# A streaming-encoder layer on one core: the attention values with 64 weight columns, and part of a depthwise convolution as packed matrix products

## The chip, the cores and the metric

The kernel runs on one core of one Trainium2 chip. The metric is device time in microseconds (us) of one execution. A core has five engines with a queue each: TensorE (PE) for matrix products into PSUM banks, with its weight loads (PEld) listed apart; VectorE (DVE), ScalarE (ACT) and GpSimd (POOL) for elementwise work; and SyncE (SP), which issues most DMAs. Each engine takes its own instructions in order and waits on semaphores of the others. A PSUM bank is 128 partitions by 512 float32; of the eight, seven rotate under the name `ps` and one, `cv`, is the accumulator of a convolution.

## What is computed

The reference has 2 layers on 512 tokens of width 1024. A layer is a SwiGLU, a mixing block, and a second SwiGLU. The change is in the mixing block, which has an attention branch and a convolution branch:

```python
probs = jax.nn.softmax(scores, axis=-1)            # 8 heads, causal by chunks of 64 tokens
outs.append(jnp.einsum('bhqk,bhkd->bqhd', probs, vs))   # 64 values per head
...
a, g = u_raw[..., :CONV_W], u_raw[..., CONV_W:]    # CONV_W = 512 channels
u = a * jax.nn.sigmoid(g)
y = lax.conv_general_dilated(u, conv_w[:, None, :], window_strides=(1,),
        padding=[(CONV_K - 1, 0)], feature_group_count=CONV_W)   # CONV_K = 31 taps per channel
return jax.nn.silu(layer_norm(y + conv_b, ln_g, ln_b))
...
x = x + jnp.concatenate([attn, conv], axis=-1) @ w_out
```

All of it is float32 in and out, to float32 accuracy.

## The kernel before

Large products are made float32-accurate by splitting each operand into a rounded part (`fp32r`) and the rest, and adding three products of these (`mm3`, L154 to L156). Products of plain float32 operands appear as two matmul records each in the trace. Activations lie with features on partitions and tokens along the row, as tiles of 128x512.

The mixing block (`mix_body`) is written as stages. First the projections, in the order of `SEQ`: gated linear units for the four convolution groups c0 to c3 (`conv_in` and `glu`, L626 to L632, each leaving a tile `u[c]` of 128 channels by 512 tokens), latents for queries and keys, then the up-projections. In `SEQ` the keys (`uk`, DVE lines L777 to L785) stand ahead of c2 and c3. Then the attention goes in steps: in a step one head's q and k are transposed (`turn`, L811 and L816), another head's scores are made and exponentiated (`scores`, L834 to L840), another's probabilities are transposed (`turn_p`, L855 and L858), another's values are summed (`values`, L868), and finished pairs of heads are transposed back (`turn_out`, L886) and split for the output projection. In `values` the transposed probabilities are the weights (128 columns) and the 64 value columns stream past them: 10 products per head, then one DVE multiplication by the reciprocal sums for a pair of heads (L875).

The convolution has 4 groups of 128 channels with 31 taps each. `CONV = "DAAD"` gives groups 0 and 3 to DVE alone: 30 fused multiply-adds into the PSUM bank `cv` (L922), then an ACT copy to `u[c]`. Groups 1 and 2 go to ACT and POOL: ACT makes each tap's product (`pr`, L926) and POOL adds it to a sum `y` (L930). From tap 16 of group 1 on, these additions are issued only after the keys. POOL then sums the four groups (L944 to L946), TensorE takes their mean (L948), and the layer norm follows on DVE, ACT and POOL up to the products of the output projection. Its attention rows for the first three output tiles (`early_groups`, `WOG = 3`) run on TensorE meanwhile.

The order of instructions on an engine is set by a scheduler: it takes the program as written, with `tc.issue_after` as extra bounds, and places each instruction by its own estimate of times. So moving an instruction in the source can move others on its queue.

Of the kernel before, what the change touches and what calls it, by code (L numbers as in the profile page):

```python
# [7 lines left out]
FP = mybir.dt.float32  # L8
# [10 lines left out]
L = 2  # L19
# [27 lines left out]
GLUP = 0  # L47
EARLY = "s"
PRELOAD = 1
E1 = 0  # L50
YP = 1
E2 = 2
E3 = 3
WOG = 3
WAKE = 10
KS = (0, 2, 4, 6, 1, 3, 5, 7)
WOP = 4
# [2 lines left out]
JOINED = ("b21", "t3", "t4")  # L60

VECS = [("g1", 8), ("gm", 8), ("g2", 8), ("gp", 8), ("gql", 3), ("gkl", 2),
        ("cw", 4 * CK), ("cb", 4), ("lg", 4), ("lb", 4), ("gq", 1), ("gk", 1)]
VOFF = {}
_o = 0
for _n, _w in VECS:
# [1 line left out]
    _o += _w  # L68
VN = _o
CCOS, CSIN, CID = 0, 64, 128  # L70
CN = 256


@with_exitstack
def encoder_kernel(ctx: ExitStack, tc: tile.TileContext, xT, consts, vecs, rgain, wgu1, wd1, wdq1,
# [54 lines left out]
    def vv(l, name):  # L130
        o, w = VOFF[name]
        return vec[:, l, o:o + w]
# [483 lines left out]

    def mix_body(kpool, l, gx, norm, done):
        u, order = [], {}

        def kept(dt=FP):  # L620
            return kpool.tile([P, S], dt, tag="m", name=nm("m"), bufs=2 * WIDE)
        ys = [None if kind == "D" else kpool.tile([P, S], FP, tag="y", name=nm("y"), bufs=2) for kind in CONV]

        def glu(pa, pg):
            tg = tmp()
            V.tensor_tensor(tg, pg, R, ALU.mult)  # L626
            sg = tmp()
            order["gate"] = A.activation(sg, tg, AF.Sigmoid).ins
            ta = tmp()
            V.tensor_tensor(ta, pa, R, ALU.mult)  # L630
            uc = kept()
            (G if GLUP else V).tensor_tensor(uc, ta, sg, ALU.mult)  # L632
            u.append(uc)

        def conv_in(c):
            pp = []
            for j in range(2):
                ps = bank()
                group(ps, load_w(wcv[l, 2 * c + j], WC, f"c{c}"), gx, range(KD), KD)
                pp.append(ps)  # L640
            glu(*pp)

        gql, gkl = vv(l, "gql"), vv(l, "gkl")
        KW = KVL + DR
# [21 lines left out]
        def latent_k():  # L666

            pk = [bank() for _ in range(NT)]
            for k0 in range(0, KD, 3):
                n = min(3, KD - k0)  # L670
                wh, wl = load_w(wkl[l, :, k0 * KW:(k0 + n) * KW], n * KW, "k")
                for k in range(k0, k0 + n):
                    cs = slice((k - k0) * KW, (k - k0 + 1) * KW)
                    for t in range(NT):
                        ts_ = slice(t * P, (t + 1) * P)
                        mm3(pk[t][:, :KW], gx[k][0][:, ts_], gx[k][1][:, ts_], wh[:, cs], wl[:, cs],
                            k == 0, k == KD - 1)
            for t in range(NT):
                A.copy(ckl[t // 2][:, t % 2], pk[t][:, :KVL])
                A.copy(cke[:, t], pk[t][:, KVL:KW])  # L680
                j = tmp()
                A.activation(j[:, :KVL], pk[t][:, :KVL], AF.Square, accum_out=ssl[:, t:t + 1])
                j = tmp()
                A.activation(j[:, :DR], pk[t][:, KVL:KW], AF.Square, accum_out=sspe[:, t:t + 1])


        tabs = []
# [173 lines left out]
        def values(h):  # L861

            if h % 2 == 0:
                heads[h]["po"] = bank()
            po = heads[h - h % 2]["po"].rearrange("p (t h d) -> p t h d", t=NT, h=2)
            for t in range(NT):
                for j in range(t + 1):
                    T.matmul(po[:, t, h % 2], heads[h]["pt"][j][:, (t - j) * P:(t - j + 1) * P],  # L868
                             vs[j][:, h * DV:(h + 1) * DV], start=j == 0, stop=j == t)
            if h % 2 == 0:  # L870
                return
            rs = small.tile([P, NT, 2], FP, tag="rs", name=nm("rs"))
            V.reciprocal(rs, heads[h - 1]["sums"])
            o = tmp()
            V.tensor_tensor(o.rearrange("p (t h d) -> p t h d", t=NT, h=2), po,  # L875
                            rs[:, :, :, None].to_broadcast([P, NT, 2, DV]), ALU.mult)
            heads[h]["o"] = o

        def turn_out(h):

            if h % 2 == 0:
                return
            o = heads[h]["o"]
            ps = bank()
            for t in range(NT):
                T.transpose(ps[:, t * P:(t + 1) * P], o[:, t * P:(t + 1) * P], ident)  # L886
# [15 lines left out]
        with tc.issue_after(order["gate"]):  # L902
            scores(0)
        for step in range(H + 6):
            for stage, lag in STAGES:
# [8 lines left out]
        for c in range(4):  # L914
            kind = CONV[c]
            acc = psum.tile([P, S], FP, tag="cv", name=nm("cv"), bufs=1) if kind == "D" else ys[c]
            tap = lambda k: cw[:, c * CK + k:c * CK + k + 1]
            A.activation(acc, u[c], AF.Identity, scale=tap(CK - 1), bias=cb[:, c:c + 1])  # L918
            for k in range(CK - 2, -1, -1):
                s = CK - 1 - k  # L920
                if kind == "D":
                    V.scalar_tensor_tensor(acc[:, s:], u[c][:, :S - s], tap(k), acc[:, s:], ALU.mult, ALU.add)  # L922
                    continue
                pr = kpool.tile([P, S], FP, tag="pr", name=nm("pr"), bufs=3)
                if kind == "A":
                    A.activation(pr[:, s:], u[c][:, :S - s], AF.Copy, scale=tap(k))  # L926
                else:
                    G.tensor_scalar(pr[:, s:], u[c][:, :S - s], tap(k), None, ALU.mult)
                with tc.issue_after(order["keys"]) if s >= PAUSE or c > 1 else nullcontext():
                    order["conv"] = G.tensor_tensor(acc[:, s:], acc[:, s:], pr[:, s:], ALU.add).ins  # L930
            if kind == "D":
                A.copy(u[c], acc)
                ys[c] = u[c]
        early = []

        def early_groups(ms):
# [3 lines left out]
                    group(early[m], wo[m], at, range(4), KD)  # L940

        early_groups(range(E1))
        ysum = tmp()
        G.tensor_tensor(ysum, ys[0], ys[1], ALU.add)  # L944
        G.tensor_tensor(ysum, ysum, ys[2], ALU.add)
        (G if YP else V).tensor_tensor(ysum, ysum, ys[3], ALU.add)  # L946
        pm = bank()
        T.matmul(pm, onesm, ysum, start=True, stop=True)  # L948
        if PRELOAD:
# [291 lines left out]
```

## Time and profile before

| what | value |
|---|---|
| median of 3 runs | 1799.76 us (1798.87 to 1799.94) |
| the profiled execution, and its span | 1798.87 us, 1797.1 us |
| PE, PEld, DVE, ACT, POOL busy | 99%, 89%, 83%, 62%, 23% of the span |
| mixing block from the end of the c3 products to the first convolution product of the output projection | 442.4 to 521.4 us (layer 0), 1332 to 1411 us (layer 1) |
| TensorE clock granted | 1.00 throughout |

A matmul row of the timeline gives start and length of one or several records. Since products overlap in TensorE's pipeline, the distance from one start to the next, and not the listed length, is what a product takes. In a row `out<-in,in` of a matmul the first operand streams and the second is the weights.

### The profile page before, as it was taken

How to read it: one execution, taken by the hardware profiler on the slowest of the kernel's cores; microseconds unless marked ns; L12 is line 12 of the kernel's file. 1: busy time of each engine (PE TensorE's matmuls, PEld its weight loads, DVE VectorE, ACT ScalarE, POOL GpSimd, SP SyncE). 2: the span in 40 equal slices, each digit the busy share in tenths (PEclk: the TensorE clock that was granted, in tenths of full speed). 3: DMA queues.
4: the chain of work that ended last, by engine and by line, in shares of the span. 5: the costliest groups of instructions: out<-in, count | busy, mean ns of one | idle time of the engine just before them, and what ended most of it. 6: DMA issues, size and time to landing. Idle time of an engine off the chain costs nothing.

```text
span 1797.1 us, 29235 instructions
## 1 busy us (share of the span) xinstructions
PE 1781.8 (99%) x11334; PEld 1602.4 (89%) x11334; DVE 1494.5 (83%) x2299; ACT 1107.5 (62%) x1721; POOL 421.5 (23%) x343
## 2 busy tenths in 40 slices
PE   9999999999999999999999999999999999999998
PEld 7899999888788899999888999998978788999997
DVE  7898988589956989898779989876998668989883
ACT  5575756457953575756645757554779435756564
POOL 1000000258943000000310000002689410000002
PEclk9999999999999999999999999999999999999999
DMA  5657575325103466665426575743250125575742
GB/s 168 171 131 182 135 177 123 109 88 134 33 22 102 123 164 161 155 160 132 123 65 170 122 194 122 193 112 111 81 147 7 46 82 160 140 183 134 182 117 74
DMA packets 70413, 226.16 MB, mean 126 GB/s; under 512 B 7937, under 2 KB 8321, under 8 KB 70273
## 3 DMA queue, kind: packets, MB, share of 16 engines
q1 hardware_dynamic: 54000, 169.74, 30.3%
q0 software_dynamic: 16128, 54.53, 18.0%
q8 instruction: 89, 1.46, 0.3%
q14 instruction: 52, 0.42, 0.1%
q10 hardware_dynamic: 144, 0.00, 0.0%
HBM read 222.15 MB, written 2.10 MB: 125 GB/s over the span
## 4 chain that ended last, share of the span: by engine, by line
PE 91%; ACT 3%; DVE 2%; POOL 2%; issue 1%; DMA 0%; SPq 0%; ACTq 0%; POOLq 0%; DVEq 0%
PE ps L154 24%; PE ps L156 23%; PE ps L155 23%; PE ps L373 11%; PE ps L374 6%; PE ps L868 1%; PE ps L834 1%; POOL y L930 1%; ACT pr L926 1%; ACT r L840 1%; PE ps L855 1%; PE ps L198 0%; POOL sck L173 0%; PE ps L217 0%; DVE wl L246 0%
## 5 line engine op out<-in xcount | busy, mean ns | idle before, releaser
L155 PE MATMUL ps<-r,wh 128*128 128x256 f32 (+1 forms) x2540 | 806.8, 318 | 0.0
L154 PE MATMUL ps<-r,wh 128*128 128x256 f32 (+1 forms) x2540 | 803.6, 320 | 2.2 <-ACT wh L138 0.7
L156 PE MATMUL ps<-r,wl 128*128 128x256 f32 (+1 forms) x2348 | 749.2, 321 | 0.0
L154 PEld LDWEIGHTS ps<-r,wh 128*128 128x128 f32 x2540 | 480.5, 189 | 47.0 <-ACT wh L138 3.6
L155 PEld LDWEIGHTS ps<-r,wh 128*128 128x128 f32 x2540 | 481.6, 190 | 35.8 <-DVE r L162 1.5
L156 PEld LDWEIGHTS ps<-r,wl 128*128 128x128 f32 x2348 | 445.1, 190 | 33.5 <-DVE wl L144 0.4
L373 PE MATMUL ps<-xj,wh 128*128 128x512 f32 x864 | 303.9, 392 | 0.0
L138 ACT CAST wh<-raw 128x1024 fp32r<-128x1024 f32 (+3 forms) x148 | 131.9, 899 | 208.1 <-PE ps L155 125.8
L390 POOL DMA_DIRECT2D ls<-in_wgu x72 | 62.7, 871 | 734.7 <-ACT ls L389 595.3
L244 ACT CAST wh<-fr 128x1024 fp32r<-128x1024 f32 (+1 forms) x160 | 157.6, 985 | 104.4 <-DVE fr L410 53.2
L144 DVE TENSOR_TENSOR wl<-raw,wh 128x1024 fp32r<-128x1024 f32 (+3 forms) x132 | 145.3, 1108 | 91.3 <-ACT wh L138 90.9
L246 DVE TENSOR_TENSOR wl<-fr,wh 128x1024 fp32r<-128x1024 f32 (+1 forms) x160 | 182.3, 1139 | 20.3 <-ACT wh L244 20.3
L373 PEld LDWEIGHTS ps<-xj,wh 128*128 128x128 f32 x864 | 161.4, 188 | 30.1
L930 POOL TENSOR_TENSOR y<-y,pr 128x511 f32<-128x511 f32 (+14 forms) x120 | 158.6, 1322 | 54.5 <-ACT pr L926 47.1
L374 PE MATMUL ps<-xj,ls 128*128 128x256 f32 x576 | 161.3, 280 | 0.0
L244 ACT CAST wh<-raw 128x1024 fp32r<-128x1024 f32 (+1 forms) x100 | 98.2, 982 | 45.1 <-PE ps L155 24.2
L246 DVE TENSOR_TENSOR wl<-raw,wh 128x1024 fp32r<-128x1024 f32 (+1 forms) x100 | 113.5, 1135 | 14.2 <-ACT wh L244 13.7
L191 POOL TENSOR_TENSOR r<-r,t 128x512 f32<-128x512 f32 x45 | 75.0, 1676 | 175.6 <-ACT t L187 174.8
L374 PEld LDWEIGHTS ps<-xj,ls 128*128 128x128 f32 x576 | 108.3, 188 | 0.0
L389 ACT ACTIVATE ls<-fr 128x1024 fp32r<-128x1024 f32 (+1 forms) x56 | 56.1, 1002 | 74.5 <-PE ps L374 42.8
L926 ACT ACTIVATE pr<-m,vec 128x511 f32<-128x511 f32 (+14 forms) x120 | 85.7, 736 | 13.2 <-POOL y L930 13.2
L922 DVE SCALAR_TENSOR_TENSOR cv<-m,vec,cv 128x511 f32<-128x511 f32 (+14 forms) x120 | 87.8, 732 | 3.6 <-ACT cv L918 2.2
(241 smaller groups left out, 2944.9 us busy)
## 6 DMA issues: line engine op xcount, KB each, us to landing
fr<-in_wgu SPq DMA_DIRECT2D x112, 512.0 KB, 4.2
ls<-in_wgu POOLq DMA_DIRECT2D x72, 512.0 KB, 6.2
raw<-in_wgu SPq DMA_DIRECT2D x62, 512.0 KB, 4.5
fr<-in_wdq SPq DMA_DIRECT2D x48, 384.0 KB, 4.6
ls<-in_wdq POOLq DMA_DIRECT2D x32, 384.0 KB, 4.8
raw<-in_wd SPq DMA_DIRECT2D x32, 384.0 KB, 3.2
raw<-in_wd SPq DMA_DIRECT2D x32, 256.0 KB, 2.8
raw<-in_wcv SPq DMA_DIRECT2D x16, 512.0 KB, 3.6
```

The source lines that it names most:

```text
L138: order["cast"] = A.copy(hi[:, :w], raw[:, :w]).ins
L144: (G if kind in POOLW.split() else V).tensor_tensor(lo[:, :w], raw[:, :w], hi[:, :w].bitcast(FP), ALU.subtract)
L154: T.matmul(o, lh, rh, start=first, stop=False, skip_group_check=free)
L155: T.matmul(o, lh, rl, start=False, stop=False, skip_group_check=free)
L156: order["mm"] = T.matmul(o, ll, rh, start=False, stop=last, skip_group_check=free).ins
L244: A.copy(hi[:, :w], src[:, :w])
L246: order["lo"] = V.tensor_tensor(lo[:, :w], src[:, :w], hi[:, :w].bitcast(FP), ALU.subtract).ins
L373: T.matmul(o, w[0][:, c], both, start=start and k == 0, stop=False, skip_group_check=True)
L374: last = T.matmul(o[:, 0:HS], w[1][:, c], both[:, 0:HS], start=False, stop=k == 3, skip_group_check=True).ins
L922: V.scalar_tensor_tensor(acc[:, s:], u[c][:, :S - s], tap(k), acc[:, s:], ALU.mult, ALU.add)
L926: A.activation(pr[:, s:], u[c][:, :S - s], AF.Copy, scale=tap(k))
L930: order["conv"] = G.tensor_tensor(acc[:, s:], acc[:, s:], pr[:, s:], ALU.add).ins
```

## The change

There are three parts.

*Values.* The weights are now the 64 value columns of a head (`vs`), and the transposed probabilities stream: 4 products per head, with 512, 384, 256 and 128 columns. Both heads of a pair write one PSUM bank, one head to partitions 0 to 63 and the other to 64 to 127, and their products alternate. The result comes out with features on partitions, so the back-transposes (`turn_out`'s, L886) go. The reciprocal sums then lie along the wrong axis; 8 products per pair of heads, with the sums broadcast to 64 weight columns and the identity streaming, spread them over a second bank, ACT copies it to SBUF, and one DVE multiplication scales the pair.

*Taps shared.* `TAPS = (14, 12, 31, 0)` gives the taps of a group that ACT and POOL add up; DVE does the others in `cv`, whose first tap is an ACT product, and one DVE addition joins both. Group 0 has 13 ACT/POOL taps and 16 DVE ones, group 1 has 11 and 18, group 2 has all 30 on ACT/POOL as before. The four groups are now summed on DVE as they come (`ysum`). From tap 5 on (`HELD`), the ACT products of groups 1 and 2 are issued only after the key latents.

*Taps on TensorE.* Of group 3, taps 0 to 15 become matrix products (`conv_pe`), and DVE keeps 14. For each 32 channels, DMA makes a tile of four copies of these channels shifted by 0 to 3 tokens (16 DMAs of 32 partitions, SBUF to SBUF, on SP's queue). The weights are four stacked 32x32 diagonals with the taps, made by POOL (L624 of the changed kernel). Each product contracts 128 rows, so four taps at once, into 32 partitions of one bank: 16 products, over four column tiles, which ACT copies out with the bias. They stand in the program ahead of attention step 3 (`PSTEP`).

Also, four early output tiles instead of three (`WOG = 4`), the first of them ahead of the mean (`E1 = 1`).

```diff
-CONV = "DAAD"
+TAPS = (14, 12, 31, 0)
+HELD = 5
+Q = 32
+PT = 16
+PSTEP = 3
...
+        diag = kpool.tile([P, PT, Q], FP, tag="m", name=nm("m"), bufs=9)
+        G.tensor_tensor(diag, cst[:, None, CI32:CI32 + Q].to_broadcast([P, PT, Q]),
+                        vv(l, "cp")[:, :, None].to_broadcast([P, PT, Q]), ALU.mult)
...
+            for i in range(4):
+                v = slot()
+                V.memset(v[:, 0:4], 0.0)
+                for r in range(4):
+                    nc.sync.dma_start(out=v[r * Q:(r + 1) * Q, r:], in_=u[c][i * Q:(i + 1) * Q, 0:S - r])
+                shifted.append(v)
...
+            for a in range(PT // 4):
+                for i in range(4):
+                    T.matmul(ps[i * Q:(i + 1) * Q, 4 * a:], diag[:, 4 * a + i], shifted[i][:, 0:S - 4 * a],
+                             start=a == 0, stop=a == PT // 4 - 1)
+            A.activation(shifted[0], ps, AF.Identity, bias=vv(l, "cb")[:, 3:4])
...
-                    T.matmul(po[:, t, h % 2], heads[h]["pt"][j][:, (t - j) * P:(t - j + 1) * P],
-                             vs[j][:, h * DV:(h + 1) * DV], start=j == 0, stop=j == t)
...
+                    T.matmul(pr[i * DV:(i + 1) * DV, t * P:(t + 1) * P], rs[:, t, i:i + 1].to_broadcast([P, DV]),
+                             ident, start=True, stop=True)
+            r = tmp()
+            A.copy(r, pr)
+            po = bank()
+            for j in range(NT):
+                for i in range(2):
+                    T.matmul(po[i * DV:(i + 1) * DV, j * P:], vs[j][:, (h - 1 + i) * DV:(h + i) * DV],
+                             heads[h - 1 + i]["pt"][j], start=j == 0, stop=j == NT - 1)
...
+            V.tensor_tensor(o, po, r, ALU.mult)
...
-                T.transpose(ps[:, t * P:(t + 1) * P], o[:, t * P:(t + 1) * P], ident)
-            at.append(split(ps, kept if len(at) < 2 else slot))
+            at.append(split(heads[h]["o"], slot))
```

On TensorE's queue at the end of the attention of layer 0, the kernel before has the values of the last head between two sets of back-transposes, and then the mean (L948):

```order
L886 MATMUL ps_5305<-cst,t_5273 128x128 x4
L868 MATMUL ps_5294<-m_4748,r_5276 128x64 x2
L868 MATMUL ps_5294<-m_4757,r_5283 128x64
...
L868 MATMUL ps_5294<-m_4766,r_5290 128x64
L868 MATMUL ps_5294<-m_4775,r_5283 128x64
L886 MATMUL ps_5328<-cst,t_5326 128x128 x4
L948 MATMUL ps_5617<-t_5613,onesm 128x512
L154 MATMUL ps_5621<-m_5105,wh_5339 128x512
```

In the changed kernel the same place reads as follows (L896 spreads the reciprocal sums, L903 are the values, L158 to L160 the three products of the output projection, L984 the mean):

```order
L896 MATMUL ps_5332<-cst,rs_5330 64x128 x8
L903 MATMUL ps_5343<-r_5265,m_4775 64x512
L158 MATMUL ps_5611<-r_5133,wh_5360 128x512
...
L160 MATMUL ps_5611<-r_5260,wl_5362 128x512
L984 MATMUL ps_5624<-m_4059,onesm 128x512
L903 MATMUL ps_5343<-r_5308,m_4775 64x512
L903 MATMUL ps_5343<-r_5272,m_4784 64x384
L903 MATMUL ps_5343<-r_5315,m_4784 64x384
```

The transposes are gone, the two heads alternate, and the mean now stands ahead of the last pair's values, with six early products in between.

Early in the attention of layer 0, the queue before has, after the scores of heads 0 and 1:

```order
L834 MATMUL ps_4817<-r_4737,r_4730 128x512
...
L811 MATMUL ps_4838<-cst,q_3853 96x128 x4
L816 MATMUL ps_4845<-cst,kn_3854 96x128 x4
L834 MATMUL ps_4852<-r_4813,r_4806 128x128
```

There the changed kernel (L860 for the scores, L837 and L842 for q and k) has its products with the diagonals, L664: three of them apart, then thirteen in a row.

```order
L860 MATMUL ps_4844<-r_4764,r_4757 128x512
...
L664 MATMUL ps_4865<-r_4706,m_3846 32x512
L837 MATMUL ps_4883<-cst,q_3856 96x128 x4
L664 MATMUL ps_4865<-r_4712,m_3846 32x512
L842 MATMUL ps_4890<-cst,kn_3857 96x128 x4
...
L664 MATMUL ps_4865<-r_4718,m_3846 32x512
...
L664 MATMUL ps_4865<-r_4724,m_3846 32x512
L664 MATMUL ps_4865<-r_4706,m_3846 32x508
```

Scores and transposes that followed directly now stand behind products that wait for the shifted copies (the tiles r_4706 to r_4724).

On DVE, around the keys of layer 0, the queue before holds no convolution work:

```order
L777 TENSOR_REDUCE ssk_3861<-t_4535 128x8
L778 TENSOR_SCALAR ssk_3861<-ssk_3861,ckc_3858 128x8 x2
L777 TENSOR_REDUCE ssk_3861<-t_4553 128x8
L758 TENSOR_TENSOR q_3853<-q_3853,scq_4442 128x768
L144 TENSOR_TENSOR wl_4709<-raw_4705,wh_4707 128x1024
L758 TENSOR_TENSOR q_3853<-q_3853,scq_4473 128x768
```

In the changed kernel (L803 and L804 are the sums of squares of the keys, L784 the scaling of the queries, L148 the splitting of a weight), group 1's last tap stands ahead of them, its joining addition L970 in their midst, and the sum of groups 0 and 1, L973, soon after:

```order
L958 SCALAR_TENSOR_TENSOR cv_5445<-m_4059,vec,cv_5445 128x482
L803 TENSOR_REDUCE ssk_3864<-t_4520 128x8
...
L970 TENSOR_TENSOR y_3849<-y_3849,cv_5445 128x500
L148 TENSOR_TENSOR wl_4736<-raw_4732,wh_4734 128x1024
...
L784 TENSOR_TENSOR q_3856<-q_3856,scq_4445 128x768
L804 TENSOR_SCALAR ssk_3864<-ssk_3864,ckc_3861 128x8
L973 TENSOR_TENSOR m_4059<-y_3848,y_3849 128x512
```

Two additions and the tail of group 1's taps have come in between the steps that make the keys ready for TensorE.

More of the change, by code (lines that the diff above doesn't have):

```diff
@@ L70 @@
 CCOS, CSIN, CID = 0, 64, 128
-CN = 256
+CI32 = 256
+CN = 288
 @with_exitstack
@@ L931, in mix_body @@
-            if kind == "D":
+                    order["conv"] = G.tensor_tensor(ys[c][:, s:], ys[c][:, s:], pr[:, s:], ALU.add).ins
+            if not n:
                 A.copy(u[c], acc)
                 ys[c] = u[c]
+            elif n < CK:
+                V.tensor_tensor(ys[c][:, n:], ys[c][:, n:], acc[:, n:], ALU.add)
+            if c:
+                last, ysum = ysum or ys[0], u[1]
+                V.tensor_tensor(ysum, last, ys[c] if n else acc, ALU.add)
         early = []
@@ L1219 @@
     consts[:, CID:CID + P] = np.eye(P, dtype=f32)
+    consts[:, CI32:CI32 + Q] = np.tile(np.eye(Q, dtype=f32), (4, 1))
     arrays = {
```

70 lines of the change are left out of this document (37 added, 33 removed).

## The prediction

> **What bounds the kernel now.** I read the page's engine lines and chain first, then the waits of TensorE over the whole span, then the windows of the only stretch the change touches much, the mixing block from the last c3 product to the first convolution product of the output projection, once per layer.
>
> ```profile
> PE 1781.8 (99%) x11334; PEld 1602.4 (89%) x11334; DVE 1494.5 (83%) x2299; ACT 1107.5 (62%) x1721; POOL 421.5 (23%) x343
> PE 91%; ACT 3%; DVE 2%; POOL 2%; issue 1%; DMA 0%; SPq 0%; ACTq 0%; POOLq 0%; DVEq 0%
> ...
> PE ps L834 <- ACT r L840: 2.7, 6, 0.7
> PE ps L886 <- DVE t L875: 1.6, 2, 0.8
> ...
> PE ps L811 <- ACT r L840: 0.5, 2, 0.3
> ...
> PE ps L948 <- POOL t L946: 0.4, 1, 0.4
> PE ps L816 <- DVE kn L785: 0.2, 1, 0.2
> ```
>
> ```profile
> 385.00:400.00 15.00, 15.00 (x106) 14.49 (x105) 13.71 (x18) 9.92 (x17) 14.53 (x11) 1.00 0.33 97
> 400.00:415.00 15.00, 14.98 (x93) 14.63 (x93) 14.05 (x33) 14.76 (x48) 12.61 (x12) 1.00 0.23 70
> 415.00:430.00 15.00, 15.00 (x69) 12.43 (x68) 15.00 (x28) 10.19 (x17) 10.53 (x8) 1.00 0.49 137
> 430.00:442.40 12.40, 12.40 (x56) 10.25 (x55) 10.93 (x19) 6.36 (x8) 12.32 (x9) 1.00 0.56 130
> 450.00:460.00 10.00, 8.75 (x47) 5.33 (x46) 10.00 (x21) 10.00 (x24) 9.53 (x9) 1.00 0.59 126
> 460.00:470.00 10.00, 9.33 (x67) 7.12 (x65) 9.84 (x20) 10.00 (x28) 8.36 (x8) 1.00 0.01 2
> 442.40:521.40 79.00, 76.23 (x501) 61.66 (x499) 64.71 (x118) 64.42 (x144) 59.59 (x49) 1.00 0.18 41
> 1332.00:1411.00 79.00, 76.23 (x502) 61.65 (x499) 64.63 (x119) 64.48 (x143) 59.40 (x49) 1.00 0.17 40
> ```
>
> A window row gives the stretch, its length, then busy time of PE, PEld, DVE, ACT and POOL. TensorE sets the time nearly everywhere; in the two stretches it idles 79.00 - 76.23 = 2.77 us each, 5.5 us together, and the waits above account for 5.4 of them. The idle lies early (450 to 470), where ACT is full and DVE almost, and at the last pair of heads. So the gain can be this idle time, plus or minus whatever the change does to TensorE's own work. Relief of DVE, ACT or POOL beyond that is worth nothing.
>
> **What TensorE's products cost.** Distances between starts in the timeline:
>
> ```profile
> 475.07 1.26 PE L855 MATMUL ps<-cst,r 128*128 128x128 f32 x10
> 476.17 0.60 PE L834 MATMUL ps<-r,r 96*128 96x256 f32 x2
> 476.60 0.19 PE L835 MATMUL ps<-mneg,mrow 128*128 128x64 bf16 x1
> 476.63 0.62 PE L811 MATMUL ps<-cst,q 128*96 128x128 f32 x4
> ...
> 477.52 0.39 PE L834 MATMUL ps<-r,r 96*128 96x128 f32 x2
> 477.75 0.19 PE L835 MATMUL ps<-mneg,mrow 128*128 128x64 bf16 x1
> 477.78 0.89 PE L834 MATMUL ps<-r,r 96*128 96x384 f32 x2
> 478.50 0.19 PE L835 MATMUL ps<-mneg,mrow 128*128 128x64 bf16 x1
> 478.54 1.10 PE L834 MATMUL ps<-r,r 96*128 96x512 f32 x2
> 479.48 0.20 PE L835 MATMUL ps<-mneg,mrow 128*128 128x64 bf16 x1
> ...
> 501.16 2.34 PE L868 MATMUL ps<-m,r 128*128 128x64 f32 x20
> 503.34 0.60 PE L886 MATMUL ps<-cst,t 128*128 128x128 f32 x4
> 503.78 2.34 PE L868 MATMUL ps<-m,r 128*128 128x64 f32 x20
> ```
>
> A float32 product is two records. It takes 0.94 us with 512 streaming columns, 0.72 with 384, 0.43 with 256, 0.23 with 128. A head's ten values products take 2.18 us (501.16 to 503.34), so 0.218 each with 64 columns, as long as with 128: there the weights set the pace, not the columns. Four back-transposes take 0.44.
>
> *Removed*, per layer: 8 heads x 2.18 = 17.4, and 4 x 0.44 = 1.8; 19.2, or 38.4 in both layers.
>
> *Added, if products run one after another:* values, 0.94 + 0.72 + 0.43 + 0.23 = 2.32 per head, 18.6 per layer; spreading the sums, 32 x 0.23 = 7.4; convolution, 16 products of 512 to 500 columns at 0.93 = 14.9. That is 40.9 per layer, 81.8 in all. A net loss of 43.4 us.
>
> *Added, if column tiles overlap.* No product before uses part of the columns, so the trace does not show this; the price lies between the above and the tile count's share of it. Values and spreading alternate over two tiles: half, 13.0 per layer. Of the convolution, three products stand apart among full-width ones (2.8) and thirteen in a row over four tiles: 13 x 0.93 / 4 = 3.0, or twice that, 6.0, if only two ever run together. I take the shares of a half and a quarter, since each tile has its own columns, weights and output partitions, and the streamed operands are different SBUF rows of the same kind as before. Net per layer: 13.0 + 5.8 - 19.2 = -0.4; **-0.8 us** for both.
>
> *Switches between tile shapes.* The queue has 20 runs of tiled products, 40 switches. Nearest row: changing from float32 to the bf16 mask product costs 0.03 (476.60 to 476.63); the upper bound is a product's tail behind the next start, 0.39 listed against 0.23 spacing:
>
> ```profile
> 508.73 0.39 PE L156 MATMUL ps<-m,wl 128*128 128x512 f32 x1
> 508.96 0.40 PE L154 MATMUL ps<-m,wh 128*128 128x512 f32 x1
> ```
>
> So 0 to 0.16 each; I take 0.03, **+1.2 us**, up to 6.4. [...]
>
> *Idle time.* The 1.6 us before L886 go with the transposes, since early products now stand there; the 0.4 before the mean go with POOL's three sums. The 3.2 us on ACT's exponentials depend on ACT's load. From its exponential table load on, ACT's queue holds 39 tap products before and 27 after:
>
> ```profile
> L926 ACT ACTIVATE pr<-m,vec 128x511 f32<-128x511 f32 (+14 forms) x120 | 85.7, 736 | 13.2 <-POOL y L930 13.2
> L922 DVE SCALAR_TENSOR_TENSOR cv<-m,vec,cv 128x511 f32<-128x511 f32 (+14 forms) x120 | 87.8, 732 | 3.6 <-ACT cv L918 2.2
> L930 POOL TENSOR_TENSOR y<-y,pr 128x511 f32<-128x511 f32 (+14 forms) x120 | 158.6, 1322 | 54.5 <-ACT pr L926 47.1
> ```
>
> 12 x 0.74 = 8.8 us less, against four copies and an eviction at no more than 0.74 each, 3.7 us. ACT comes out 5 us lighter, DVE loses 16 of group 3's 30 multiply-adds (11.7 us), POOL 12 of 39 additions and the three sums. I recover 4.6 of the 5.5 us: **-4.6 us**, bounds 0 and -5.5.
>
> *Keys.* Before the attention DVE gets more: 34 multiply-adds instead of 30, two joins and one sum, 7 x 0.73 = 5.1 us per layer. Its idle time from 385 to 442.4 is 1.29 + 0.95 + 0 + 1.47 = 3.7. So 1.4 us do not fit. TensorE already waited once for the last scaled keys (L816, 0.2). I take 0.5 per layer, **+1.0 us**, bounds 0 and 2.8.
>
> *Hidden.* The shifted copies: the tile they read is made by 448.8, SP takes 0.33 per issue, a 512 KB load lands in 3.6.
>
> ```profile
> 446.44 2.37 DVE L632 TENSOR_TENSOR m<-t,t 128x512 f32<-128x512 f32 x1 [1.18 <-ACT t L628]
> 386.25 0.33 SPq L136 DMA_DIRECT2D raw<-in_wuq  x1
> raw<-in_wcv SPq DMA_DIRECT2D x16, 512.0 KB, 3.6
> 460.35 0.19 PE L835 MATMUL ps<-mneg,mrow 128*128 128x64 bf16 x1
> ```
>
> The fourth tile's copies land about 448.8 + 16 x 0.33 + 3.6 = 457.7. TensorE wants it behind head 2's 512-column scores, which end near 460.4 before and later with three products ahead. The two weight loads moved behind these issues on SP serve the second half of the output projection, past 521.4. The diagonals (one POOL operation, made during the previous SwiGLU's end), the four small memsets and the fourth early tile (12 products moved, none added) cost nothing; POOL's cover is its idle time, and if it were gone the norm of the mixing block would wait 1.3 us.
>
> **The sum.** -0.8 + 1.2 - 4.6 + 1.0 = -3.2 on the profiled execution's 1798.87: 1795.7 us. That execution is 0.9 below the median of the runs.
>
> **Rivals.** (B) *Tiles overlap only one pass deep.* The two records of a product need the same tile one after the other, so if starts keep their order, the next tile can run beside the second record alone: a half also for the convolution, 3.0 more per layer, 1801.7. For it: the records of a product always stand together in the timeline. Against: nothing seen. [...]
>
> (C) *No overlap:* +43.4 of products, and the rest as above, less the -0.8: 1795.7 + 44.2 = 1839.9. It is the slower case by one mechanism, on TensorE's queue in the attention; it decides once the added products take over 38.4 + 3.2 = 41.6 us, that is if overlap saves less than half of 81.8.
>
> (D) *Late keys.* If all 5.1 us of added DVE work delay the keys, TensorE waits 5.1 per layer instead of the 0.5 taken: +9.2, 1804.9. For it: DVE is 15.00 of 15.00 busy at 415 to 430. Against: 3.7 us of idle around it.
>
> (E) *Late copies.* Every microsecond past TensorE's turn costs one per layer, all of the attention being queued behind it. With landings three times as long (10.8), 4 us late: 1803.7. For it: the DMA engines are 0.59 busy with weights at 450 to 460. Against: the margin of 2.7 us above.
>
> **How the numbers follow.** The likeliest case has 56 in 100, with its own range 1788 (the three single products packed too, all idle recovered) to 1802 (drains at the upper bound); B 18, D 10, E 10, C 6. Under 0.2% (3.6 us) is about what measurement cannot tell from none. Faster: 48 of the likeliest, 4 of B, 1 of D: 0.53. Same: 7, 9, 2 and 2 of E: 0.20. Slower: the remaining 27. The range 1787 to 1807 takes in B, D and E at their prices, and leaves out C and the ends.
>
> **What the changed profile would show.** Right: rows of L903 and L664 whose starts lie closer than the distances above, half and a quarter; the waits on L886 gone and those on ACT's exponentials below 1 us. B: thirteen L664 products over 6 us; C: over 12. D: a wait of L842 on DVE's keys. E: a wait of L664 on a DMA. What I do not price, a buffer freed later because the shifted tiles hold four of the 35 slots, would make the prediction wrong in yet another way.

## The result, and the profile after

The changed kernel is slower: 1818.73 us median (1817.83 to 1821.14, 4 runs) against 1799.51 us (4 runs) of the kernel before, a ratio of 1.0109 with a 95% interval of 1.0092 to 1.0127. The prediction was 1795.7 us, with a range up to 1807. The profiled execution has a span of 1819.0 us, 21.9 more than that of before; it is the slowest of its four runs and that of before the fastest of its own, so this is 2.7 more than the difference of the medians.

The engine line on the page of the changed kernel:

```profile
PE 1790.3 (98%) x11302; PEld 1584.5 (87%) x11302; DVE 1491.5 (82%) x2295; ACT 1115.1 (61%) x1723; POOL 401.3 (22%) x327
```

Its waits of TensorE over the whole span (us in total, times, longest):

```profile
PE ps L160 <- DVE wl L148: 4.6, 2, 2.6
PE ps L158 <- ACT r L165: 2.9, 2, 1.4
PE ps L842 <- DVE kn L811: 2.4, 1, 2.4
PE ps L158 <- ACT t L773: 2.2, 2, 1.2
PE ps L881 <- DVE r L844: 2.0, 2, 1.0
PE ps L664 <- DMA r<-m: 1.9, 1, 1.9
...
PE ps L860 <- ACT r L866: 0.3, 1, 0.3
```

L148 makes the low part of a weight, L773 squares the queries, L811 scales the keys, L664 is the convolution's products, L165 splits rows for the output projection, and L844 copies the transposed k out of its PSUM bank. The waits on the exponentials (L866) and on the back-transposes are gone, as forecast, but longer ones have come, and most of them are on VectorE and lie ahead of the attention. The rows below give the places in time, first from the timeline of the kernel before and then from that of the changed kernel. They are the first scores and the first convolution product of the output projection in layer 0, then the same two in layer 1; the changed kernel's rows begin with its wait for the keys.

```profile
449.68 0.38 PE L834 MATMUL ps<-r,r 96*128 96x128 f32 x2
521.45 1.20 PE L154 MATMUL ps<-r,wh 128*128 128x512 f32 x4
1339.70 0.39 PE L834 MATMUL ps<-r,r 96*128 96x128 f32 x2
1411.46 1.20 PE L154 MATMUL ps<-r,wh 128*128 128x512 f32 x4
```

```profile
453.61 0.42 PE L842 MATMUL ps<-cst,kn 128*96 128x128 f32 x2 [2.45 <-DVE kn L811]
460.98 0.38 PE L860 MATMUL ps<-r,r 96*128 96x128 f32 x2
533.86 1.20 PE L158 MATMUL ps<-r,wh 128*128 128x512 f32 x4 [1.45 <-ACT r L165]
1357.92 0.39 PE L860 MATMUL ps<-r,r 96*128 96x128 f32 x2
1433.53 1.20 PE L158 MATMUL ps<-r,wh 128*128 128x512 f32 x4 [1.45 <-ACT r L165]
```

The first scores come 11.3 us later in layer 0. From the scores to the convolution product it was 71.8 us and is 72.9. From there to the scores of layer 1, 5.8 us are lost. In layer 1 the attention goes from 71.8 to 75.6, and from there to the end it is 385.6 and 385.5 us. So 11.3 + 5.8 = 17.1 of the 21.9 us lie **ahead** of the two attentions, where the sharing of the taps has changed VectorE's queue, and 1.1 + 3.9 = 5.0 lie in them. The fourth early tile moved nothing across these places: in both kernels each of the three lines of the output projection has 16 products in the attention, so four tiles of twelve (first L154 of before, then L158 of the changed kernel).

```profile
449.60:521.40 71.80, 7.20 (x16) 3.01 (x16) 1.00 0.09 20
460.90:532.50 71.60, 6.80 (x16) 3.01 (x16) 1.00 0.12 28
```

The windows ahead of the attention of layer 0 (stretch, length, busy time of PE, PEld, DVE, ACT, POOL, then the granted clock), to be held against the rows of before at 400 to 442:

```profile
400.00:415.00 15.00, 15.00 (x95) 14.80 (x95) 14.68 (x29) 12.14 (x41) 10.30 (x11) 1.00 0.31 97
415.00:430.00 15.00, 10.77 (x40) 7.69 (x39) 15.00 (x27) 10.09 (x19) 10.10 (x7) 0.91 0.11 33
423.80:427.20 3.40, 0.73 (x2) 0.30 (x2) 3.40 (x6) 3.27 (x7) 1.65 (x1) 1.00 0.00 0
427.30:430.60 3.30, 3.15 (x7) 2.48 (x8) 3.30 (x8) 0.60 (x1) 2.54 (x1) 0.50 0.60 181
```

VectorE has no gap, as before, but TensorE loses 4.23 us of 15. And after it had idled (0.73 us busy of 3.40), its granted clock was 0.50 for 3.4 us. Three such stretches lie within the span (near 427, 455 and 1328); none did before, apart from the last 3 us in both kernels. As an estimate from the 0.50, each takes at most half its length, 1.7 us, so 5.1 together.

What stands in VectorE's queue there: multiply-adds of group 1 (L958) between the sums of squares (L774), the rotation and the weights. Of before, the last multiply-add ahead of the keys:

```profile
405.69 0.71 DVE L922 SCALAR_TENSOR_TENSOR cv<-m,vec,cv 128x482 f32<-128x482 f32 x1
```

and the changed kernel from 416 on:

```profile
416.61 0.72 DVE L958 SCALAR_TENSOR_TENSOR cv<-m,vec,cv 128x486 f32<-128x486 f32 x1
...
421.87 0.54 DVE L774 TENSOR_REDUCE ssh<-t 128x4 f32<-128x384 f32 x1
422.33 0.71 DVE L958 SCALAR_TENSOR_TENSOR cv<-m,vec,cv 128x485 f32<-128x485 f32 x1
...
427.45 1.21 DVE L148 TENSOR_TENSOR wl<-raw,wh 128x1024 fp32r<-128x1024 f32 x1
...
434.07 0.71 DVE L958 SCALAR_TENSOR_TENSOR cv<-m,vec,cv 128x482 f32<-128x482 f32 x1
```

Before, all 30 were done at 406.4. Now nine of group 1's start between 408 and 435, 6.5 us of work, and a join and a sum follow. Four of the nine stand at 415 to 430, the one stretch where VectorE had nothing to spare.

The packing itself, in the changed kernel's timeline of layer 0 (a row's products take from its start to the next row's):

```profile
466.47 1.05 PE L664 MATMUL ps<-r,m 128*32 128x512 f32 x2
467.45 0.64 PE L837 MATMUL ps<-cst,q 128*96 128x128 f32 x4
468.02 1.04 PE L664 MATMUL ps<-r,m 128*32 128x512 f32 x2
...
473.19 3.58 PE L664 MATMUL ps<-r,m 128*32 128x512 f32 x26
476.70 0.55 PE L881 MATMUL ps<-cst,r 128*128 128x128 f32 x3
...
487.05 1.09 PE L896 MATMUL ps<-cst,rs 128*64 128x128 f32 x16
487.97 2.32 PE L903 MATMUL ps<-r,m 128*64 128x512 f32 x16
```

Thirteen products over four column tiles take 3.51 us, 0.27 each, where one alone at full width took 0.93 in the kernel before. The eight spreading products take 0.92 against 8 x 0.23 = 1.84: half. The four transposes of a head's q between two tiled products take 0.57 instead of 0.44.

### The profile page after: what moved, and what is told of

It is laid out like the page before. It is cut to its first block, busy times and chain, and to the rows that moved or that the text cites. A ratio compares the mean times of both kernels' runs of the same rounds, so it can differ in the third digit from the quotient of the medians.

```text
span 1819.0 us, 29249 instructions
## 1 busy us (share of the span) xinstructions
PE 1790.3 (98%) x11302; PEld 1584.5 (87%) x11302; DVE 1491.5 (82%) x2295; ACT 1115.1 (61%) x1723; POOL 401.3 (22%) x327
## 4 chain that ended last, share of the span: by engine, by line
PE 54%; DVE 3%; POOL 1%; issue 1%; ACT 1%; DMA 0%; ACTq 0%; POOLq 0%; DVEq 0%
PE ps L158 13%; PE ps L160 13%; PE ps L159 13%; PE ps L377 7%; PE ps L378 4%; POOL y L965 1%; PE ps L860 1%; DVE cv L958 1%; PE ps L903 1%; PE ps L881 0%; DVE wl L148 0%; PE ps L664 0%; DVE wl L250 0%; DVE r L166 0%; PE ps L202 0%
## 5 line engine op out<-in xcount | busy, mean ns | idle before, releaser
L158 PE MATMUL ps<-r,wh 128*128 128x256 f32 (+1 forms) x2572 | 817.9, 322 | 7.8 <-ACT r L165 2.9
L159 PE MATMUL ps<-r,wh 128*128 128x256 f32 (+1 forms) x2572 | 819.6, 319 | 0.0
L160 PE MATMUL ps<-r,wl 128*128 128x256 f32 (+1 forms) x2380 | 763.3, 323 | 5.7 <-DVE wl L148 4.6
L158 PEld LDWEIGHTS ps<-r,wh 128*128 128x128 f32 x2572 | 487.4, 190 | 57.0 <-ACT r L165 3.7
L159 PEld LDWEIGHTS ps<-r,wh 128*128 128x128 f32 x2572 | 488.1, 190 | 37.2 <-issue 1.9
L160 PEld LDWEIGHTS ps<-r,wl 128*128 128x128 f32 x2380 | 452.0, 190 | 42.8 <-DVE wl L148 6.2
L148 DVE TENSOR_TENSOR wl<-raw,wh 128x1024 fp32r<-128x1024 f32 (+3 forms) x132 | 146.3, 1116 | 89.1 <-ACT wh L142 88.5
L965 POOL TENSOR_TENSOR y<-y,pr 128x511 f32<-128x511 f32 (+19 forms) x108 | 145.9, 1353 | 38.9 <-ACT pr L963 33.4
L394 POOL DMA_DIRECT2D ls<-in_wdq x32 | 27.7, 865 | 263.3 <-ACT ls L393 263.3
L963 ACT ACTIVATE pr<-m,vec 128x511 f32<-128x511 f32 (+19 forms) x108 | 76.0, 725 | 14.5 <-POOL y L965 14.0
```

The lines of the kernel that those rows point to most:

```text
L148: (G if kind in POOLW.split() else V).tensor_tensor(lo[:, :w], raw[:, :w], hi[:, :w].bitcast(FP), ALU.subtract)
L158: T.matmul(o, lh, rh, start=first, stop=False, skip_group_check=free)
L159: T.matmul(o, lh, rl, start=False, stop=False, skip_group_check=free)
L160: order["mm"] = T.matmul(o, ll, rh, start=False, stop=last, skip_group_check=free).ins
L394: G.dma_start(out=lo[:, :n], in_=w, accum_op=ALU.add)
L965: order["conv"] = G.tensor_tensor(ys[c][:, s:], ys[c][:, s:], pr[:, s:], ALU.add).ins
```

## The experiments

Theory T: the sharing of the taps puts VectorE's work ahead of the keys and the rest works as forecast. Rival P: tiled products, switches or copies cost more than their rows show. Each edit is against the changed kernel unless it names another. In e1 to e4, "without" a part means that this part stands as in the kernel before; the early products stay as changed (four tiles, one ahead of the mean).

**e1, e2, e3, e4: the parts one by one.** e1 undoes the sharing alone:

```diff
-TAPS = (14, 12, 31, 0)
-HELD = 5
+TAPS = (0, 31, 31, 0)
+HELD = 99
```

e2 keeps the sharing alone, e3 the values alone, e4 the TensorE taps alone; where these are undone, `values` and `turn_out` are those of before, and group 3 has no `conv_pe` and goes wholly to VectorE.

> The changed kernel with the taps split as before (group 0 wholly on VectorE, groups 1 and 2 on ScalarE and GpSimd, nothing held back); values and the sixteen TensorE taps stay. Theory T (the sharing of groups 0 and 1 puts more work on VectorE and GpSimd ahead of the keys, and the rest of the change works as forecast): about 1796 us, between 1788 and 1803, with the first scores at 450 us in layer 0 and no waits of TensorE on the squares or on the low parts of weights between 420 and 460. Rival P (tiled products, their switches or the copies cost more than the attention's rows showed): 1814 or more.

> The sharing of groups 0 and 1 alone: values by token tiles as before, group 3 wholly on VectorE. Theory T: slower than before by 15 to 25 us (1815 to 1825), with the first scores at about 461 us. Rival P: within 4 us of before.

> Values as weight columns alone; taps split as before and group 3 wholly on VectorE. Theory T, by the starts in the changed kernel's rows (values 2.25 for eight, spreading 0.92 for eight): per layer 4 x (2 x 2.25 + 2 x 0.92 ... that is 13 us) against 19.2 removed, so 6 us less per layer and 1787 us, if the four copies on ScalarE per layer stay hidden, and up to 1794 if not. Rival P: 1800 or more.

> Sixteen taps of group 3 on TensorE alone; values as before, taps of groups 0 to 2 as before. Theory T: TensorE gets 5.8 us per layer, VectorE loses 11.7 of work in the attention, which bounds nothing there: 1799.5 + 11.6 - 0 to 5 = 1806 to 1811. Rival P: 1815 or more.

Measured: e1 1806.76 (ratio 1.0041, 1.0026 to 1.0056), e2 1811.63 (1.0069, 1.0054 to 1.0084), e3 1799.10 (0.9998, 0.9988 to 1.0007), e4 1813.00 (1.0079, 1.0062 to 1.0096). e2 is 12.4 us slower than the kernel before, and the changed kernel 12.0 slower than e1: T's cause is there. The 12.4 are not all the sharing's, since e2 keeps the early products of the change; by its profile about 10 us lie ahead of the two attentions. With the sharing alone the first scores of layer 0 start at 457.16, 7.5 us late (11.3 in the changed kernel, so the other parts add to it). In e1 the first scores start at 449.77 and the waits on weights are gone. But e1, e3 and e4 lie 4, 5 and 2 us above T's ranges (and e2 3 below its own), and all of them show one cause, here in e1's waits of TensorE:

```profile
PE ps L202 <- DVE r L195: 3.4, 2, 1.7
```

Behind the mean, TensorE waits 1.7 us per layer for the layer norm's squares, which it did not in the kernel before; a double stretch of half clock (6.8 us; e1's mean granted clock is 0.997) follows the second of these waits, and none the first. T was incomplete, and by their totals alone e3 and e4 lie as near to P's figures as to T's; what speaks against P is the rows above, in which the tiled products take close to what was forecast.

**e5: group 1 behind the keys.** VectorE keeps all its multiply-adds, but those of group 1 are queued behind the last scaled key.

```diff
-                V.tensor_tensor(kn[:, t, :, DN:DQ], cke[:, t, None, :].to_broadcast([P, H, DR]),
-                                scp[:, :, None].to_broadcast([P, H, DR]), ALU.mult)
+                order["keyed"] = V.tensor_tensor(kn[:, t, :, DN:DQ], cke[:, t, None, :].to_broadcast([P, H, DR]),
+                                scp[:, :, None].to_broadcast([P, H, DR]), ALU.mult).ins
...
-            for s in range(n or 1, CK):
+            with tc.issue_after(order["keyed"]) if c == 1 else nullcontext():
+              for s in range(n or 1, CK):
```

> The changed kernel with VectorE's multiply-adds of convolution group 1 (18 per layer, and so its join) queued behind the last scaled key. Theory T1 (those about twenty operations, 14 us, stand in VectorE's queue between 408 and 435 where it has no idle time, and push the queries' and keys' work back): first scores at 450 to 452 in layer 0 instead of 461, no waits of TensorE on the low parts of weights or the squares between 420 and 445, and 1800 to 1806 in all. Rival T2 (the additions on GpSimd, which stretch VectorE's operations beside them, do it): they stay where they were, so 1812 or more.

Measured: 1809.83 (1.0056, 1.0041 to 1.0071), 8.9 us less than the changed kernel; the forecast of 1800 to 1806 was missed. The place is settled all the same. The window and the first scores of e5:

```profile
415.00:430.00 15.00, 15.00 (x68) 12.39 (x67) 15.00 (x26) 9.86 (x16) 11.55 (x10) 1.00 0.38 111
```

```profile
450.98 0.39 PE L860 MATMUL ps<-r,r 96*128 96x128 f32 x2
...
462.12 1.88 PE L664 MATMUL ps<-r,m 128*32 128x512 f32 x2 [2.96 <-DMA r<-m]
```

TensorE idles no longer at 415 to 430, and the scores start 10 us sooner, with GpSimd busier than in the changed kernel (11.55 of 15.00 against 10.10). That speaks against the rival of GpSimd stretching VectorE's work as the main cause. Between the attentions another 6.2 us come back, so 16.2 of the 17.1 us. What keeps the total up is new: the attention of layer 0 takes 78.5 us instead of 72.9. TensorE now reaches the tiled products before the copies have landed, and waits 2.96 us for one, and a stretch of half clock begins at the end of that wait (the product there is listed at 1.88 us, 1.05 in the changed kernel). In layer 0 of the changed kernel, where TensorE was late itself, it did not wait for the copies.

**e6: the table loaded once.** In the changed kernel the sum of the groups is ready earlier, and ScalarE's early load of the SiLU table runs before the last exponentials. The exponentials load their own table again, and the SiLU loads its table once more behind the mean. ACT's timeline of the changed kernel:

```profile
502.46 1.28 ACT L986 ACT_TABLE_LOAD   x1
503.98 1.28 ACT L866 ACT_TABLE_LOAD   x1
...
530.48 1.28 ACT L1002 ACT_TABLE_LOAD   x1 [7.92 <-DVE t L1000]
```

```diff
-            A.activation(tiny("pre", 1), ysum[:, 0:1], AF.Silu)
+            with tc.issue_after(heads[H - 1]["e", 1]), tc.issue_after(heads[H - 1]["e", 3]):
+                A.activation(tiny("pre", 1), ysum[:, 0:1], AF.Silu)
```

> The changed kernel with the early load of ScalarE's SiLU table queued behind the last exponentials of the last head, so that it is not loaded before them, lost and loaded again. If the second loading is on the path behind the mean (wait of 1.45 of TensorE on the split rows, once per layer): about 3 us less, 1815 to 1817. If that wait has another cause: 1818 to 1820.

Measured: 1816.25 (1.0089, 1.0072 to 1.0106), 2.5 us less, and the two waits of 1.45 on the split rows (L165) are gone. So the table was about 2.5 us of the loss; the size is rough, since in the profile of e6 other waits differ too (1.00 us for the copies is new in layer 0).

**e7, e8: the early products as before**, on e3 and on e1.

```diff
-E1 = 1
-WOG = 4
+E1 = 0
+WOG = 3
```

> Values as weight columns alone (as in e3) with the early products placed as before: three tiles, none ahead of the mean, two between the mean and the sums of squares. Theory T3 (in e3 the gain of the values was eaten behind the mean: with one tile there, TensorE waits 1.7 us per layer for the squares, and the granted clock falls to a half for 3.4 us right after, 1.7 us more): both go, and 1799.1 - 3.1 - 3.4 gives 1792 to 1794. Rival: the values save nothing in themselves, the waits only move: 1798 to 1800.

> e1 (values and sixteen TensorE taps, taps of groups 0 to 2 split as before) with the early products placed as before. T3: the 3.4 us of waits behind the mean and the 3.4 us of half clock go: 1806.8 - 6.8 gives 1799 to 1802. Rival: 1805 to 1808.

Measured: e8 1799.71 (1.0003, 0.9994 to 1.0012), 7.1 us less than e1, as forecast: the waits at L202 and the half clock are gone (its mean granted clock is 1.000, e1's 0.997). e7 1800.76 (1.0007, 0.9997 to 1.0016): nothing gained on e3, and the theory T3 of its expectation fell there. The squares are on time now, but the mean itself is late, on its sum L948 (`PE ps L959 <- DVE m L948: 8.1, 2, 4.8`). Behind the longer of the two waits, in layer 1, the products are 0.43 apart instead of 0.23:

```profile
1398.55 2.04 PE L959 MATMUL ps<-m,onesm 128*128 128x512 f32 x2 [4.79 <-DVE m L948]
...
1400.82 0.63 PE L159 MATMUL ps<-r,wh 128*128 128x512 f32 x1
1401.24 0.63 PE L160 MATMUL ps<-r,wl 128*128 128x512 f32 x1
```

So shorter values alone end in a wait: TensorE gets through the attention sooner, and the convolution is not ready for the mean.

**e9, e11: fewer taps, and all taps in one row.** e9 is e7 with eight TensorE taps, e11 is e8 with its sixteen products in one row.

```diff
-PT = 16
-PSTEP = 3
+PT = 8        # e9; e11 keeps 16
+PSTEP = 4
```

> e7 (values as weight columns, old split of the taps, early products as before) with eight taps of group 3 on TensorE, all eight in a row one step later. In e7 the mean waits 4.1 us per layer for VectorE's multiply-adds of group 3, and three stretches of half clock follow (5.1 us in all). Seven fewer multiply-adds are 5.1 us per layer, so the mean should be on time; eight products at a quarter, with switches, add 2.1 per layer: 1800.8 - 8.1 - 5.1 + 4.2 = 1791.8, between 1789 and 1796. Rival (the attention is bound by ScalarE and VectorE together, so that what TensorE saves comes back as waits): 1797 to 1801.

> e8 (1799.7) with the sixteen tap products in one row, one step later: three singles (2.8 us) become 0.7 of the row, and the wait for the copies (1.3 in layer 1) goes: 1799.7 - 4.2 - 1.3 = 1794.2, between 1792 and 1798. Rival (what TensorE saves comes back as waits on ScalarE's exponentials): 1798 to 1801.

Measured: e9 1800.11 (1.0001, 0.9992 to 1.0010), a miss; e11 **1795.05** (0.9976, 0.9967 to 0.9986), as forecast, and faster than both kernels. In e11 the row is sixteen products in 4.15 us, 0.26 each, and no copy is waited for:

```profile
462.52 4.23 PE L664 MATMUL ps<-r,m 128*32 128x512 f32 x32 [0.33 <-ACT r L866]
466.67 0.64 PE L837 MATMUL ps<-cst,q 128*96 128x128 f32 x4
```

In e9 the mean still waits, 2.92 and 3.9 us, although VectorE has fewer multiply-adds. The sum of the groups waits for GpSimd's additions of group 2, of which nine stand in a row at 1.36 us (GpSimd, then VectorE, of e9):

```profile
491.39 12.28 POOL L965 TENSOR_TENSOR y<-y,pr 128x490 f32<-128x490 f32 x9
```

```profile
503.71 0.69 DVE L973 TENSOR_TENSOR m<-m,y 128x512 f32<-128x512 f32 x1 [1.09 <-POOL y L965]
```

**e10, e14: is it the waiting that lowers the clock?** Both add throwaway products ahead of the mean in e7. In e10 (four) nothing fixed their place; in e14 (three) they stand behind the last values product, and the early products behind the mean.

```diff
+        with tc.issue_after(order["val"]):
+            for _ in range(3):
+                T.matmul(pm, onesm, vs[0], start=True, stop=True)
```

> e7 with four throwaway products (full width, results overwritten, output unchanged) ahead of the product with the mean, 3.8 us per layer, in the time in which TensorE waits there. If the half clock follows from that waiting: no such stretch within the kernel, and 1800.8 - 5.1 = 1795.7, 1794 to 1798. If it comes from elsewhere: stretches stay, 1800 to 1803.

> e7 with three throwaway products (2.8 us per layer, results overwritten) behind the last values product, where TensorE waits 3.3 and 4.8 us for the mean; the early products stay behind the mean. If the half clock follows from the waiting: the three stretches (10.2 us of half clock, 5.1 us lost) go, 1795 to 1797. If filling does not prevent them: 1800 to 1802.

Measured: e10 1806.90 (1.0040, 1.0026 to 1.0053). The throwaway products went ahead of the last values and delayed them, so it says little. TensorE waited for the squares instead, and a stretch of 6.8 us at half clock lay at the wait of 1.71 us in layer 0, but none behind the longer one of 2.3 in layer 1 (by the mean granted clock, 0.998). e14 1797.22 (0.9991, 0.9982 to 0.9999), 3.5 us less than e7 with more work. In layer 0 the products behind the mean are at full pace:

```profile
502.13 2.84 PE L961 MATMUL ps<-m,onesm 128*128 128x512 f32 x6
505.43 1.12 PE L962 MATMUL ps<-m,onesm 128*128 128x512 f32 x2 [0.45 <-DVE m L948]
...
506.62 0.40 PE L159 MATMUL ps<-r,wh 128*128 128x512 f32 x1
506.86 0.39 PE L160 MATMUL ps<-r,wl 128*128 128x512 f32 x1
```

In layer 1, where 1.9 us of waiting were left over, one stretch of 3.4 us remains (the mean granted clock is 0.999, 0.996 in e7). So of the three stretches of e7 (one in layer 0, two in a row in layer 1) two went with the waiting.

**e12, e13, e16: GpSimd's row.** e12 (on e11) and e13 (on e9) give VectorE the last six taps of group 2, behind the keys as in e5. e16 (on e9) leaves those six additions out, so its result lacks six taps.

```diff
-TAPS = (0, 31, 31, 0)
+TAPS = (0, 31, 25, 0)      # e12, e13
...
+                if c == 2 and s >= 25:      # e16
+                    continue
                 with tc.issue_after(order["keys"]) if s >= PAUSE or c > 1 else nullcontext():
```

> e11 (1795.05) with the last six taps of group 2 on VectorE behind the last scaled key instead of on ScalarE and GpSimd: six additions fewer (8 us) in GpSimd's row ahead of the mean. Theory T4 (GpSimd's row sets the start of the product with the mean): the wait there (1.3 us) goes and the attention shortens by 1 to 2 us per layer, 1791 to 1794. Rival (ScalarE and VectorE bound it): 1795 or more.

> e9 (1800.1) with the same six taps of group 2 on VectorE behind the last scaled key. T4: in e9 the mean waits 6.9 us in both layers for GpSimd's row, and two stretches of half clock follow (3.4); eight us less in that row takes both away, 1800.1 - 10.3 = 1789.8, up to 1794 if VectorE (five multiply-adds and a join more, 4.4 us) is late next. Rival (VectorE's load is what is late): 1799 or more.

> e9 (1800.1) with the last six additions of group 2 on GpSimd left out in each layer (8 us; ScalarE still makes the products, six taps are missing from the result); nothing else is changed. T4 (the mean waits for GpSimd's row): the waits of 3.0 and 3.9 us at the mean and both stretches of half clock (3.4 us in all) go, 1800.1 - 10.3 = 1789.8, 1788 to 1793. Rival (VectorE's own queue is as late): 1796 to 1800.

Measured: e12 1817.16 (1.0101, 1.0085 to 1.0116) and e13 1829.23 (1.0168, 1.0154 to 1.0182), far off. There is one accumulator `cv`: group 3's multiply-adds cannot start before group 2's are joined, and the join waits for the additions. In e12 it comes at 495.92, fourteen multiply-adds follow it, and the mean waits 9.08 us (17.26 in e13, both in layer 0). These two tell nothing of GpSimd's row. e16 does: 1798.58 (0.9996, 0.9987 to 1.0005). In layer 0 the row ends at 495.9 instead of 503.7, and the mean no longer waits in either layer, so it was the row that it waited for. But only 1.5 us of the 10 came back. The scheduler put most of the last pair's values behind the mean, singly between full-width products, and TensorE waits about 1 us per layer for the squares instead. How the rest divides was not settled.

**e15: the whole change in another order**: the edits of e5, e6, e8 and e11 together, all 16 + 18 + 14 multiply-adds still on VectorE.

> The whole change, with group 1's multiply-adds behind the last scaled key (e5), the table loaded once (e6), the early products as before (e8) and the sixteen products in a row (e11). If the sharing costs only by its place: 1808.9 of e5, less 2.5 (table), less 3 (wait for the copies), less 4.2 (row) gives about 1799, and 1793 to 1800 with the half clock gone. If its load costs wherever it stands: 1802 or more.

Measured: 1797.46 (0.9991, 0.9982 to 1.0000), 21.3 us less than the changed kernel with not one product or tap fewer, and level with the kernel before to slightly faster. Its first scores in layer 0:

```profile
450.70 0.38 PE L860 MATMUL ps<-r,r 96*128 96x128 f32 x2
```

The profiled executions by stages, in us, with the places that the rows of the result name:

| kernel | up to the first scores | attention, layer 0 | up to the scores of layer 1 | attention, layer 1 | rest |
|---|---|---|---|---|---|
| before | 449.7 | 71.8 | 818.2 | 71.8 | 385.6 |
| changed | 461.0 | 72.9 | 824.1 | 75.6 | 385.5 |
| e1, old taps | 449.8 | 75.2 | 818.7 | 77.4 | 385.4 |
| e5, group 1 behind the keys | 451.0 | 78.5 | 817.8 | 74.9 | 385.6 |
| e8, e1 with the old early products | 449.7 | 72.3 | 818.0 | 71.8 | 385.5 |
| e11, e8 with one row | 449.6 | 69.7 | 817.8 | 70.3 | 385.6 |
| e15, all edits together | 450.7 | 71.2 | 817.6 | 70.5 | 385.6 |

So the loss was one of order: ahead of the attentions (first and third column) nearly all of it goes with the place of group 1's multiply-adds, and within them with the table, the early products and the row. But even behind the keys the sharing brought nothing: e15 is still 2.4 us slower than e11, which has the old split of the taps. What these 2.4 us are made of was not settled.

## Why the prediction was wrong, point by point

The step that failed is **"Keys"**: "I take 0.5 per layer, +1.0 us, bounds 0 and 2.8". The delay is 11.3 us ahead of the attention of layer 0 and 5.8 ahead of that of layer 1, 17.1 instead of 1.0. The step set the added operations of the whole stretch 385 to 442 against its idle time there (5.1 against 3.7). But the row it had quoted, 15.00 of 15.00 busy at 415 to 430, has no idle time at all, and the order put 6.5 us of multiply-adds between 408 and 435, four of nine into that row, where before had none. Also, the price was a wait on the keys alone. In the run TensorE waited on the late squares too (ScalarE's square at 422.44 had itself waited 2.58 us for VectorE's sum, L774), and on the late low parts of weights, and each of the three longest of these waits came with a stretch of half clock (3.4 us at 0.50), which no row of before could show. Rival D named the mechanism and the sign, with a tenth of the chance, and its 1804.9 had the same ceiling of 5.1 us per layer. The signs that the prediction had named for D and E both appear: L842 waits on the keys (2.4) and L664 on a DMA (1.9).

The second step that failed is **"Idle time"**, with what the text hid or priced at nothing: for the two attentions the sum had -0.8 + 1.2 - 4.6 = -4.2 us, and they take 5.0 more. The points below take this apart.

*Products and packing* (-0.8): right in mechanism and near in size. Per layer 4 x (0.92 + 2.25) = 12.7 for values and spreading (13.0 predicted) and 3 x 0.98 + 3.51 = 6.4 for the convolution (5.8), against 19.2 removed, so -0.1 per layer where -0.4 was forecast. Rivals B and C are out: 0.27 per product, in a row of two-record products over four tiles, is 3.4 times as fast as one alone (0.93).

*Switches* (+1.2, at most 6.4): within the bounds, above the value taken. The transposes between tiled products show 0.13 too much for a pair of switches at 467.45, a single tiled product 0.04 (0.98 for 0.94). That a switch drains TensorE, as the 1802 of the likeliest case has it, no run shows; these two rows are what the runs showed in its place.

*Idle time* (-4.6): not had. The waits named did go (0.3 is left on the exponentials), but others took their place: 2.0 us of the probabilities' transposes on VectorE's copy of the transposed k (L881 on L844), 2.9 on the split rows that the table made late, and 1.9 on the copies.

*Hidden.* The copies were not hidden once TensorE was on time (e1, e5), so rival E was half right, at 1 to 3 us. The early products, priced at nothing as "12 products moved", cost 7 us between e1 and e8: none moved past the first convolution product, four tiles having stood ahead of it already, but one tile fewer stands between the mean and the squares. Of the table's second loading the text had nothing.

## What to carry to other kernels

Load and idle time over a long window do not price work that is added to an in-order queue: count what stands in the queue between the two operations that somebody waits for. Where a change moves cover (early products, a preload, a transfer), ask at each of these places what becomes late if everything else is on time, since delays elsewhere can hide it. A wait of TensorE should be priced with the half clock that may follow it, here 3.4 us at 0.50 at the waits of 2.02 to 2.62 in the changed kernel and 6.7 at the one of 4.79 in e7.

## What the runs showed of the hardware that was not expected

*The clock.* In the records of the changed kernel the granted clock within the span is 1.00 or 0.50, and its three stretches at 0.50 are 3.41 us each. They start 27.3 and 873.8 us apart, 8 and 256 such lengths. In e7 the clock was 0.50 for at least 6.7 us without a break (1397.3 to 1404.0). The three of the changed kernel began 1.8 us into a wait of TensorE of 2.02, 0.95 us behind the end of one of 2.45, and 2.3 us into one of 2.62; in e16 one began 2.4 us behind the end of a wait of 0.95. Of the waits of 2.6 us and more, each that the rows of a run show had products at half pace behind it (as 0.43 us apart instead of 0.23): 2.62 in the changed kernel, 3.01 in e2, 2.96 in e5, 3.29 and 4.79 in e7, 2.92 in e9, 9.08 in e12 and 17.26 in e13. So had some of those between 0.95 and 2.45, while others of that size had none (2.3 in e10, 1.94 in the changed kernel, 1.70 in e1). What falls into the wait itself costs nothing, as the first 1.2 us of the 6.7 in e7, whose wait ended at 1398.55. In e4 a wait of 1.41 us was enough:

```profile
1416.59 1.02 PE L202 MATMUL ps<-ones,r 128*128 128x1 f32 x8 [1.41 <-DVE r L195]
```

```profile
1414.40:1417.80 3.40, 1.99 (x14) 1.51 (x13) 1.99 (x4) 0.52 (x1) 0.00 (x0) 1.00 0.00 0
1418.00:1421.20 3.20, 3.20 (x9) 2.42 (x9) 0.69 (x1) 0.00 (x0) 0.92 (x1) 0.50 0.00 0
```

The 3.4 us ahead of the stretch are 59% busy, so TensorE had not idled throughout them. What sets the start and the length of a stretch was not shown.

*VectorE beside GpSimd.* A key scaling that takes 0.70 us otherwise took 3.45 beside GpSimd's additions (VectorE, then GpSimd, of the changed kernel):

```profile
448.70 3.45 DVE L809 TENSOR_TENSOR kn<-kn,sck 128x512 f32<-128x512 f32 x1
```

```profile
449.68 3.60 POOL L965 TENSOR_TENSOR y<-y,pr 128x511 f32<-128x511 f32 x2
```

Behind it the other part of the same key (L811) took 1.48 us instead of 0.43, and TensorE waits 2.45 us for that at 453.61, so at this one place the stretching, 3.8 us for both, accounts for the wait. What made both longer these rows do not show: the key scaling started 0.98 us ahead of the additions, while GpSimd was issuing two DMAs.
